# A hybrid decoder layer on one core: the values product of the attention emitted one piece later, and the gate rows' last steps moved behind the attention

## The chip, the cores and the metric

The kernel runs on one core of one Trainium2 chip. The metric is device time in microseconds (us) of one execution, as the median of several. The profile is of one execution; its times count from its first instruction. Engine names: TensorE (PE; its weight loads are listed as PEld), VectorE (DVE), ScalarE (ACT), GpSimd (POOL) and SyncE (SP), which issues all DMAs of this kernel.

## What is computed

One decoder layer over 1024 positions of width 1024, all in 32 bits. Three mixers read the same normalised input: a stick-breaking attention with 8 heads of 64, an mLSTM with 4 heads of 128 in chunks of 128, and a cross-attention into 256 memory tokens. Their outputs are merged by gates and projected, and a gated MLP with a short convolution follows. The change touches the first two:

```python
# stick-breaking attention, one block of 128 queries
z = einsum('bhtd,bhsd->bhts', q[t0:t1], k[:t1]) * scale
log_fail = where(strict, log_sigmoid(-z), 0.0)
log_after = cumsum(log_fail, axis=3, reverse=True) - log_fail
w = where(strict, exp(log_sigmoid(z) + log_after), 0.0)
out = einsum('bhts,bhsd->bhtd', w, v[:t1])
# mLSTM: for each chunk, from the gates i and log f
b = cumsum(lfc);  m_inter = b + m_st
m_t = maximum(m_inter, max(log_d, axis=-1));  w_inter = exp(m_inter - m_t)
m_new = maximum(b_last + m_st, max(b_last - b + ic))
```

## The kernel before

The program is written as Python generators, and a scheduler places the emitted instructions on each engine by the order of emission and by which buffers are free. Every engine then runs its own list strictly in order, so what stands in front of an instruction on its engine holds it. Positions are reversed, so that "later" keys stand at higher block numbers.

**The attention.** Four passes (`for p in range(4)`), each for a pair of heads. A pass has 12 pieces (`PIECES`): a block `rb` of 128 queries against up to four blocks of 128 keys. A piece goes through this chain:

- `sb_weights`: TensorE computes the scores into `z` (L410, L412 adds the mask, L413), two PSUM banks for both heads, one buffer. ScalarE takes two sigmoids of them (L415, L416). VectorE makes the running product by a scan for each head (L422), and multiplies (L424) to the weights `g`.
- `sb_apply`: TensorE transposes `g` block by block into `tr` (L438), ScalarE copies that to `wt` (L440, tile `y`, two buffers), and TensorE multiplies `wt` with the values (L444), accumulating over the pieces of a row of blocks. `store_y` writes four finished blocks out (L395, L396).

Between the pieces stand parts of a dense projection (`chunks`, L149 to L151: three matmuls of 512 columns for each product, since operands are split into a high and a low part): in the first three passes the queries and keys of the next pair of heads, whose evictions are L374 to L377 and L381 to L386. In two pieces of three one such part of 12 matmuls is emitted. The order within a piece is set by the loop: scores, then the part of the projection, then `sb_apply` of the piece before.

**The gate rows.** `gate_rows` computes the mLSTM's decays and maxima, which depend on the input alone, with the 8 chunks x 4 heads on 32 partitions. It is a generator of four steps. The first has the log-sigmoid, the prefix sums and running maxima (`suffix`) and writes their last columns to DRAM (`bl_d`). The second reads them back with heads on partitions (L556) and runs through the chunks, seven dependent instructions on 4 x 1 elements (L561), to `mp_d`. The third reads that back (L567), forms the stabiliser `gm` (L569) and three exponentials (L571, L573, L576), and writes two rows to `me_d` (L577, L578). The fourth transposes three of the tiles (L582) and copies them to `cols` (L583). The mLSTM's chunks (`ml_chunk`) read `me_d` (L843) and `cols` much later.

The steps are called in the attention's first two passes:

```python
            if p < 2 and n in (2, 7):
                next(rows_step)
```

**Behind the attention** come the dense units of `staged` (`seven`: a product of two pairs of weight tiles in seven multiplications). `go(n)` advances them. In them ScalarE and VectorE split each weight tile into a high and a low part (L136, L137) ahead of its 12 matmuls, in two alternating buffers, `whi` and `wlo`.

Of the kernel before, what the change touches and what calls it, by code (L numbers as in the profile page):

```python
# [12 lines left out]
AF = mybir.ActivationFunctionType  # L13
ALU = mybir.AluOpType
# [11 lines left out]
MLH, MLD = 4, 128  # L26
# [3 lines left out]
NCH = S // P  # L30
# [12 lines left out]
def tile_hybrid_layer(ctx: ExitStack, tc: tile.TileContext, xT, memT, vecs, w_t, w_n, w_kv, w_if,  # L43
# [4 lines left out]
    nc = tc.nc  # L48
# [11 lines left out]
    def nm(s):  # L60
        uid[0] += 1
        return f"{s}_{uid[0]}"
# [5 lines left out]
    def T(shape, tag, dt=F32, bufs=None):  # L68
        pool = {"mw": mlp, "mst": mlp, "ga": mlp, "gm": mlp,  "px": late[0]}.get(tag, sb)
        return pool.tile(shape, dt, tag=tag, name=nm(tag), bufs=bufs or BUFS[tag])  # L70
# [7 lines left out]
    def wide():  # L78
        return T([P, S], "U")

    def two(tag):
        return psx[0].tile([P, 2, HALF], F32, tag=tag, name=nm("ps_" + tag), bufs=1)
# [3 lines left out]
    def small(n, p=P):  # L86
        return T([p, n], "sm")

    def bank(tag):
        if tag in ("pj", "pv"):  # L90
            return ps.tile([P, HALF], F32, tag=tag, name=nm("ps_" + tag), bufs=2)
        if px1 is not None:
            if not spare.get(tag):
                t = two(tag)
                spare[tag] = [t[:, 1], t[:, 0]]
            return spare[tag].pop()
        return psx[0].tile([P, HALF], F32, tag=tag, name=nm("ps_" + tag), bufs=2)

    def dtile(shape, name):
        return dr.tile(shape, F32, tag=name, name=name)  # L100
# [4 lines left out]
    def ts(t):  # L105
        return slice(t * P, (t + 1) * P)
# [53 lines left out]
    def rstd(acc, n):  # L160

        nt = n // P
        pc = bank("tr")
        for t in range(nt):
            nc.tensor.matmul(pc[:, t:t + 1], acc[:, ts(t)], ones[:, :1], start=True, stop=True)
        return rstd_cols(pc[:, :nt], nt, D)
# [103 lines left out]
    def x_stats(xp):  # L270
        acc = []
        for i in range(4):
            sq = wide()
            nc.scalar.activation(sq, xp[i], AF.Square)
            acc.append(sq)
            if i:
                nc.vector.tensor_add(acc[0], acc[0], sq)
        a = acc[0][:, hs(0)]
        nc.vector.tensor_add(a, a, acc[0][:, hs(1)])
        return a  # L280
# [10 lines left out]
    pk, pv = [[bank(t) for _ in range(2)] for t in ("z", "pv")]  # L291
# [26 lines left out]
    r = rstd(x_stats(xp[1]), HALF)  # L318
# [74 lines left out]
    def store_y(b, j, h, src_ps):  # L393
        t = T([P, HALF], "me")
        nc.scalar.activation(t, src_ps, AF.Copy)  # L395
        nc.sync.dma_start(y_d[b][j, :, hs(h)], t)  # L396
# [5 lines left out]
    acc_pv = [None]  # L402
# [22 lines left out]
        carry[0] = f[:, :, w:w + 1]  # L425
        return g

    def sb_apply(p, rb, o, g):
        nb = NCH - rb
        m = min(4, nb - o)  # L430
        w = m * P
        if rb % 4 == 3 and o == 0:
            acc_pv[0] = bank("pv")
        pv = acc_pv[0]
        pt = two("tr")
        for a in range(2):
            for j in range(m):
                nc.tensor.transpose(pt[:, a, ts(j)], g[:, a, ts(j)], ident)  # L438
        wt = T([P, 2, HALF], "y")
        nc.scalar.activation(wt[:, :, :w], pt[:, :, :w], AF.Copy)  # L440
        for j in range(m):
            s = rb + o + j
            for a in range(2):
                nc.tensor.matmul(  # L444
                    pv[64 * a:64 * a + 64, ts(rb % 4)],
                    sbv[s // 2][:, s % 2, (2 * p + a) * 64:(2 * p + a + 1) * 64],
                    wt[:, a, ts(j)], start=(o + j == 0), stop=(o + j == nb - 1))
        if rb % 4 == 0 and o + 4 >= nb:
            store_y(0, p, rb // 4, pv)
# [39 lines left out]
    a = x_stats(xp[0])  # L489
    for _ in range(1):  # L490
        next(vals)
    r = rstd(a, HALF)
# [16 lines left out]
    R = NCH * MLH  # L509

    def rows_tile():
        return T([R, P], "mw")
# [12 lines left out]
    cols = const.tile([P, 3, R], F32, tag="cols", name="cols")  # L525

    def gate_rows():
        gi, gf = rows_tile(), rows_tile()
        for g, t in ((0, gi), (1, gf)):
            nc.sync.dma_start(t, if_d[g].rearrange("h (c t) -> c h t", t=P))  # L530

        e = rows_tile()
        nc.scalar.activation(e, gf, AF.Abs)
        nc.scalar.activation(e, e, AF.Exp, scale=-1.0)
        u = rows_tile()
        nc.vector.tensor_scalar(u, e, 1.0, None, op0=ALU.add)
        lu = rows_tile()
        nc.scalar.activation(lu, u, AF.Ln)
        nc.vector.scalar_tensor_tensor(e, u, 1.0, e, op0=ALU.subtract, op1=ALU.subtract)
        nc.vector.reciprocal(u, u)  # L540
        nc.vector.tensor_mul(e, e, u)
        nc.vector.tensor_sub(lu, lu, e)
        bcur = rows_tile()
        nc.vector.scalar_tensor_tensor(bcur, gf, 0.0, lu, op0=ALU.min, op1=ALU.subtract)

        bcum = suffix(bcur, ALU.add)
        ga = T([R, P], "ga", bufs=1)
        nc.vector.tensor_sub(ga, gi, bcum)
        amax = suffix(ga, ALU.max)
        bl_d = dtile([2, R], "bl_d")  # L550
        nc.sync.dma_start(bl_d[0].rearrange("(r o) -> r o", o=1), bcum[:, 0:1])
        nc.sync.dma_start(bl_d[1].rearrange("(r o) -> r o", o=1), amax[:, 0:1])
        yield
        last = small(16, MLH)
        for g in range(2):
            nc.sync.dma_start(last[:, 8 * g:8 * g + 8].rearrange("h (c o) -> h c o", o=1),  # L556
                              bl_d[g].rearrange("(c h o) -> h c o", h=MLH, o=1))
        mp = small(8, MLH)
        nc.vector.memset(mp, 0.0)
        for c in range(NCH - 1, 0, -1):  # L560
            nc.vector.tensor_scalar(mp[:, c - 1:c], mp[:, c:c + 1], last[:, 8 + c:9 + c], last[:, c:c + 1],  # L561
                                    op0=ALU.max, op1=ALU.add)
        mp_d = dtile([NCH, MLH], "mp_d")
        nc.sync.dma_start(mp_d.rearrange("c (h o) -> h c o", o=1), mp.rearrange("h (c o) -> h c o", o=1))
        yield
        mprev = small(1, R)
        nc.sync.dma_start(mprev, mp_d.rearrange("c (h o) -> (c h) o", o=1))  # L567
        gm = T([R, P], "gm", bufs=1)
        nc.vector.tensor_scalar(gm, amax, mprev, -1.0, op0=ALU.max, op1=ALU.mult)  # L569
        ge = rows_tile()  # L570
        nc.scalar.activation(ge, gm, AF.Exp, bias=mprev)  # L571
        gw = rows_tile()
        nc.scalar.activation(gw, ga, AF.Exp, bias=gm[:, 0:1])  # L573
        gfl = rows_tile()
        nc.vector.tensor_sub(gfl, gm, bcum)
        nc.scalar.activation(gfl, gfl, AF.Exp)  # L576
        nc.sync.dma_start(me_d[0], gm)  # L577
        nc.sync.dma_start(me_d[1], ge)  # L578
        yield
        pt = two("tr")[:, 0]  # L580
        for i, t in enumerate((ga, gw, gfl)):
            nc.tensor.transpose(pt[:, i * R:(i + 1) * R], t, ident[:R, :R])  # L582
        nc.vector.tensor_copy(cols.rearrange("p a r -> p (a r)"), pt[:, :3 * R])  # L583
        yield

    rows_step = gate_rows()


# [5 lines left out]
        nc.sync.dma_start(v_d[t], v)  # L594


    ready = []

    def apply_next():
        if ready:  # L600
            sb_apply(*ready.pop(0))

    for p in range(4):
        now = st
        if p < 3:
            st, chunks = sb_qk(p + 1)
            chunks = chunks()
        else:
            chunks = nat_chunks(1, ev_v, [0, 1, 2, 3, 7, 6, 5, 4])
        for n, (rb, o) in enumerate(PIECES):  # L610
            g = sb_weights(p, now, rb, o)
            if n % 3 < 2:
                next(chunks, None)
            if p < 2 and n in (2, 7):
                next(rows_step)
            apply_next()
            ready.append((p, rb, o, g))
        if p < 3:
            for _ in chunks:
                pass  # L620
    apply_next()

    spare.clear()
# [22 lines left out]
    def turn(i, tags):  # L646
        cyc[i] += 1
        return tags[cyc[i] % len(tags)]
# [146 lines left out]
    for g in range(2):  # L795
        for a, b, n in ((0, C_CW, 16), (32, C_CB, 4)):
            nc.vector.tensor_scalar(cw[:, a + g * n:a + (g + 1) * n], col(b + g * n, n), KAP[g], None,
                                    op0=ALU.mult)
# [118 lines left out]
    def go(n):  # L917
        for _ in range(n):
            next(dense, None)
# [4 lines left out]
            next(chunks)  # L924
    go(3)
    LONG[:], SHORT[:] = ["pj"], ["pv"]
    go(24)
    state = [[None], [None]]
    old = []
    for c in range(NCH - 1, -1, -1):  # L930
# [82 lines left out]
    for i in range(3 * KT):  # L1013
        b, n = i // KT, i % KT
# [5 lines left out]
        for h in (1, 0):  # L1020
            p = bank("pj")
            for j in range(4):
                c = slice(((n % 2) * 4 + j) * P, ((n % 2) * 4 + j + 1) * P)
# [104 lines left out]
    for j in range(2):  # L1128
        bl = x1p[2 + j]
        for i in range(2):  # L1130
            nc.vector.scalar_tensor_tensor(bl[:, hs(i)], bl[:, hs(i)], col(C_GFFN + 4 + 2 * j + i), rows,
                                           op0=ALU.mult, op1=ALU.mult)
# [11 lines left out]
    last = first[2]  # L1144
    for u in units[3:]:
# [3 lines left out]
        last = u  # L1149
# [66 lines left out]
    R = [bank(turn(2, LONG)) for _ in range(4)]  # L1216
# [169 lines left out]
```

## Time and profile before

| | |
|---|---|
| median of 3 runs | 1730.78 us (1727.46 to 1735.63) |
| profiled execution | 1730.8 us, span 1728.9 us |
| TensorE busy | 1674.0 us, 97% of the span |
| VectorE busy | 1197.5 us, 69% |
| ScalarE busy | 831.6 us, 48% |
| GpSimd busy | 63.5 us, 4% |

Busy time is the union of an engine's instructions. Matmuls are pipelined, so that two of 0.39 us can start 0.23 us apart, and a TensorE that is shown busy all the time may still lose time between them. The granted clock is the share of TensorE's full clock of 2.4 GHz. The stretch from 114 to 359 us is the attention, and the change concerns it and the 90 us behind it.

### The profile page before, as it was taken

How to read it: one execution, taken by the hardware profiler on the slowest of the kernel's cores; microseconds unless marked ns; L12 is line 12 of the kernel's file. 1: busy time of each engine (PE TensorE's matmuls, PEld its weight loads, DVE VectorE, ACT ScalarE, POOL GpSimd, SP SyncE). 2: the span in 40 equal slices, each digit the busy share in tenths (PEclk: the TensorE clock that was granted, in tenths of full speed). 3: DMA queues.
4: the chain of work that ended last, by engine and by line, in shares of the span. 5: the costliest groups of instructions: out<-in, count | busy, mean ns of one | idle time of the engine just before them, and what ended most of it. 6: DMA issues, size and time to landing. Idle time of an engine off the chain costs nothing.

```text
span 1728.9 us, 21405 instructions
## 1 busy us (share of the span) xinstructions
PE 1674.0 (97%) x7927; PEld 1339.9 (78%) x7927; DVE 1197.5 (69%) x1763; ACT 831.6 (48%) x1298; POOL 63.5 (4%) x139
## 2 busy tenths in 40 slices
PE   8997999999999999999999999999999999999999
PEld 4776777778786777777788888688888888788887
DVE  5555777686973655655546756998788777789874
ACT  4545767554554444555521334465555455544431
POOL 1000000000000121200000000000000000000000
PEclk9998999999999999999999999999999999999999
DMA  8321100162233455532475355143222221496142
GB/s 295 135 63 20 38 19 31 56 195 67 104 143 103 147 174 159 178 116 80 176 256 185 108 176 182 50 135 110 74 74 97 86 73 49 138 355 215 41 140 80
DMA packets 99069, 212.73 MB, mean 123 GB/s; under 512 B 13184, under 2 KB 41088, under 8 KB 98964
## 3 DMA queue, kind: packets, MB, share of 16 engines
q1 hardware_dynamic: 98964, 211.35, 36.6%
q8 instruction: 63, 1.03, 0.3%
q14 instruction: 42, 0.34, 0.1%
HBM read 156.71 MB, written 54.61 MB: 122 GB/s over the span
## 4 chain that ended last, share of the span: by engine, by line
PE 58%; DVE 2%; DMA 1%; ACT 1%; issue 1%; POOL 0%; POOLq 0%; SPq 0%; ACTq 0%; DVEq 0%
PE ps_pj L149 9%; PE ps_pj L151 9%; PE ps_pj L150 9%; PE ps_pv L150 4%; PE ps_pv L151 4%; PE ps_pv L149 4%; PE ps_tr L149 3%; PE ps_tr L151 3%; PE ps_tr L150 3%; PE ps_z L151 2%; PE ps_z L149 2%; PE ps_z L150 2%; PE ps_z L986 1%; PE ps_z L961 1%; DMA raw<-y_d 1%
## 5 line engine op out<-in xcount | busy, mean ns | idle before, releaser
L150 PE MATMUL ps_pj<-h,whi 128*128 128x512 f32 x620 | 244.4, 394 | 0.0
L136 ACT ACTIVATE whi<-raw 128x512 fp32r<-128x512 f32 (+1 forms) x112 | 93.6, 836 | 186.6 <-PE ps_pj L150 80.7
L149 PE MATMUL ps_pj<-h,whi 128*128 128x512 f32 x412 | 163.9, 398 | 0.1
L149 PE MATMUL ps_pj<-pg,whi 128*128 128x512 f32 x396 | 155.6, 393 | 0.0
L151 PE MATMUL ps_pj<-pg,wlo 128*128 128x512 f32 x380 | 148.4, 391 | 0.2 <-DVE wlo L137 0.2
L150 PEld LDWEIGHTS ps_pj<-h,whi 128*128 128x128 f32 x620 | 116.6, 188 | 24.4 <-issue 1.1
L151 PE MATMUL ps_pj<-h,wlo 128*128 128x512 f32 x332 | 131.6, 396 | 0.7 <-DVE wlo L137 0.7
L422 DVE TENSOR_TENSOR_SCAN U<-U 128x512 f32<-128x512 f32 (+3 forms) x96 | 88.6, 965 | 45.6 <-ACT U L415 44.8
L804 DVE SCALAR_TENSOR_TENSOR y<-U,vec,y 128x1023 f32<-128x1023 f32 x88 | 112.6, 1282 | 7.9 <-ACT y L802 7.9
L149 PEld LDWEIGHTS ps_pj<-h,whi 128*128 128x128 f32 x412 | 77.8, 189 | 16.0 <-DVE U L1029 0.8
L137 DVE TENSOR_TENSOR wlo<-raw,whi 128x1024 fp32r<-128x1024 f32 x54 | 66.0, 1222 | 32.6 <-ACT whi L136 32.5
L149 PEld LDWEIGHTS ps_pj<-pg,whi 128*128 128x128 f32 x396 | 74.6, 188 | 17.4 <-issue 1.6
L151 PEld LDWEIGHTS ps_pj<-pg,wlo 128*128 128x128 f32 x380 | 71.3, 188 | 15.7 <-DVE wlo L137 0.6
L136 ACT ACTIVATE whi<-pg 128x512 fp32r<-128x512 f32 (+1 forms) x59 | 43.4, 736 | 73.9 <-PE ps_pv L150 20.0
L150 PE MATMUL ps_pj<-pg,whi 128*128 128x512 f32 x188 | 74.7, 397 | 0.0
L151 PEld LDWEIGHTS ps_pj<-h,wlo 128*128 128x128 f32 x332 | 62.8, 189 | 14.7 <-DVE wlo L137 1.6
L137 DVE TENSOR_TENSOR whi<-raw,whi 128x512 fp32r<-128x512 f32 x58 | 40.1, 691 | 34.9 <-ACT whi L136 34.9
L150 PE MATMUL ps_pv<-h,whi 128*128 128x512 f32 x164 | 63.8, 389 | 0.0
L802 ACT ACTIVATE y<-U,vec 128x1024 f32<-128x1024 f32 x44 | 54.6, 1240 | 14.7 <-DVE U L708 14.7
L151 PE MATMUL ps_pj<-h,whi 128*128 128x512 f32 x156 | 61.4, 394 | 0.0
L415 ACT ACTIVATE U<-ps_z 128x1024 f32<-128x1024 f32 (+3 forms) x48 | 39.0, 813 | 37.1 <-PE ps_z L413 36.9
L137 DVE TENSOR_TENSOR wlo<-raw,wlo 128x512 fp32r<-128x512 f32 x58 | 40.1, 691 | 23.4 <-ACT wlo L136 23.0
(432 smaller groups left out, 4341.9 us busy)
## 6 DMA issues: line engine op xcount, KB each, us to landing
raw<-in_w_t_dram SPq DMA_DIRECT2D x29, 512.0 KB, 3.3
gate_d<-U SPq DMA_DIRECT2D x24, 512.0 KB, 2.6
U<-gate_d SPq DMA_DIRECT2D x24, 512.0 KB, 6.2
pg<-in_w_up_dram SPq DMA_DIRECT2D x22, 512.0 KB, 3.9
act_d<-y SPq DMA_DIRECT2D x22, 512.0 KB, 3.1
pg<-in_w_t_dram SPq DMA_DIRECT2D x21, 512.0 KB, 3.2
raw<-in_w_dn_dram SPq DMA_DIRECT2D x18, 512.0 KB, 4.0
raw<-in_w_o_dram SPq DMA_DIRECT2D x16, 512.0 KB, 4.1
```

The costliest lines, as they stand in the source:

```text
L136: nc.scalar.activation(hi, src, AF.Copy)
L137: (eng or nc.vector).tensor_sub(lo, src, hi.bitcast(F32))
L149: nc.tensor.matmul(out, lh, rh, start=start, stop=False, skip_group_check=more)
L150: nc.tensor.matmul(out, lh, rl, start=False, stop=False, skip_group_check=more)
L151: nc.tensor.matmul(out, ll, rh, start=False, stop=stop, skip_group_check=more)
L415: nc.scalar.activation(f[:, :, 1:w + 1], z[:, :, :w], AF.Sigmoid, scale=-0.125)
L422: nc.vector.tensor_tensor_scan(f[:, a, 1:w + 1], f[:, a, 1:w + 1], f[:, a, 1:w + 1], 1.0 if o == 0 else f[:, a, 0:1], op0=ALU.mult, op1=AL ...
L802: nc.scalar.activation(out, u, AF.Identity, bias=bias, scale=taps[0])
L804: nc.vector.scalar_tensor_tensor(out[:, :S - s], u[:, s:], taps[s], out[:, :S - s], op0=ALU.mult, op1=ALU.add)
L961: nc.tensor.matmul(z[:, i * NMEM:(i + 1) * NMEM], q[:, ts(2 * t2 + i)], kv[:, 0], start=True, stop=True)
L986: nc.tensor.matmul(pv, kv[:, 1, ts(m)], pTs[m], start=(m == 0), stop=(m == 1))
```

## The change

`sb_apply` is cut in two. `sb_turn` does the transposes and the copy, `sb_apply` the product with the values. A piece waits in one list between weights and turn, and in another between turn and product, so that its product is emitted one piece later. Of the gate rows, only step 1 is still called in the attention; steps 2 to 4 are called behind it, among the dense units. The run through the chunks, `gm` and one difference go to GpSimd, the copy to `cols` to ScalarE, and the tile that is read back moves from the small tiles to a part of a wide one.

```diff
-    def sb_apply(p, rb, o, g):
-        nb = NCH - rb
-        m = min(4, nb - o)
+    def sb_turn(rb, o, g):
+        m = min(4, NCH - rb - o)
         w = m * P
-        if rb % 4 == 3 and o == 0:
-            acc_pv[0] = bank("pv")
-        pv = acc_pv[0]
         pt = two("tr")
         for a in range(2):
             for j in range(m):
                 nc.tensor.transpose(pt[:, a, ts(j)], g[:, a, ts(j)], ident)
         wt = T([P, 2, HALF], "y")
         nc.scalar.activation(wt[:, :, :w], pt[:, :, :w], AF.Copy)
+        return wt
+
+    def sb_apply(p, rb, o, wt):
+        nb = NCH - rb
+        m = min(4, nb - o)
+        if rb % 4 == 3 and o == 0:
+            acc_pv[0] = bank("pv")
+        pv = acc_pv[0]
         for j in range(m):
...
-        last = small(16, MLH)
+        last = wide()[:MLH, :16]
...
-        nc.vector.memset(mp, 0.0)
+        nc.gpsimd.memset(mp, 0.0)
         for c in range(NCH - 1, 0, -1):
-            nc.vector.tensor_scalar(mp[:, c - 1:c], mp[:, c:c + 1], last[:, 8 + c:9 + c], last[:, c:c + 1],
+            nc.gpsimd.tensor_scalar(mp[:, c - 1:c], mp[:, c:c + 1], last[:, 8 + c:9 + c], last[:, c:c + 1],
                                     op0=ALU.max, op1=ALU.add)
...
-        nc.vector.tensor_scalar(gm, amax, mprev, -1.0, op0=ALU.max, op1=ALU.mult)
+        nc.gpsimd.tensor_scalar(gm, amax, mprev, -1.0, op0=ALU.max, op1=ALU.mult)
...
-        nc.vector.tensor_sub(gfl, gm, bcum)
+        nc.gpsimd.tensor_sub(gfl, gm, bcum)
...
-        pt = two("tr")[:, 0]
+        pt = bank("tr")
...
-        nc.vector.tensor_copy(cols.rearrange("p a r -> p (a r)"), pt[:, :3 * R])
+        nc.scalar.activation(cols.rearrange("p a r -> p (a r)"), pt[:, :3 * R], AF.Copy)
...
-    ready = []
+    weights, turned = [], []
+
+    def turn_next():
+        if weights:
+            p, rb, o, g = weights.pop(0)
+            turned.append((p, rb, o, sb_turn(rb, o, g)))
 
     def apply_next():
-        if ready:
-            sb_apply(*ready.pop(0))
+        if turned:
+            sb_apply(*turned.pop(0))
...
-            if p < 2 and n in (2, 7):
+            if (p, n) == (0, 2):
                 next(rows_step)
             apply_next()
-            ready.append((p, rb, o, g))
+            turn_next()
+            weights.append((p, rb, o, g))
...
+    apply_next()
+    turn_next()
     apply_next()
...
-    go(24)
+    next(rows_step)
+    go(8)
+    next(rows_step)
+    go(4)
+    next(rows_step)
+    go(12)
```

In the changed file the transposes are L434, the copy L436 and the product L448; the gate rows' read back is L560, the steps through the chunks L565, the second read back L571, the exponentials L575, L577 and L580.

The first place is TensorE's list in the first pass, around the product of its third piece. `ps_tr` holds the transposes, `ps_z` scores, `ps_pj` the projection, `ps_pv` the products with the values from `y`. Before:

```order
L438 MATMUL ps_tr_1032<-ident,U_922 128x128 x6
L410 MATMUL ps_z_1047<-pg_274,pg_272 128x512
L412 MATMUL ps_z_1047<-mask,ident 128x128
L413 MATMUL ps_z_1047<-pg_276,pg_272 128x512
L410 MATMUL ps_z_1047<-pg_275,pg_273 128x512
L444 MATMUL ps_pv_906<-y_1039,pg_548 64x128 x2
L444 MATMUL ps_pv_906<-y_1039,pg_436 64x128 x4
L412 MATMUL ps_z_1047<-mask,ident 128x128
L413 MATMUL ps_z_1047<-pg_277,pg_273 128x512
L149 MATMUL ps_pj_1019<-h_105,whi_858 128x512
```

The product stood four matmuls behind the transposes that it needs, between the scores of a later piece. The same product (`y_1039`) after the change:

```order
L150 MATMUL ps_pj_1015<-h_115,whi_858 128x512
L151 MATMUL ps_pj_1015<-h_107,wlo_859 128x512
L149 MATMUL ps_pj_1015<-h_108,whi_858 128x512
L150 MATMUL ps_pj_1015<-h_116,whi_858 128x512
L151 MATMUL ps_pj_1015<-h_108,wlo_859 128x512
L448 MATMUL ps_pv_990<-y_1039,pg_548 64x128 x2
L448 MATMUL ps_pv_990<-y_1039,pg_436 64x128 x4
L434 MATMUL ps_tr_1078<-ident,U_1008 128x128 x8
L410 MATMUL ps_z_1089<-pg_274,pg_272 128x128
```

It now stands behind all six matmuls of those scores and 12 of the projection, the last five of which are shown, and just ahead of the next piece's transposes.

The second place is SP's list behind the attention, after the change. `w_t` are weights of the dense units, `bl_d`, `mp_d` and `me_d` the gate rows' DRAM tiles:

```order
L691 DMA pg_3163<-in_w_t_dram 128x1024
L560 DMA U_3204<-bl_d 4x8x1 x2
L568 DMA mp_d<-sm_3207 4x8x1
L571 DMA sm_3609<-mp_d 32x1
L581 DMA me_d<-gm_3611 32x128
L582 DMA me_d<-mw_3613 32x128
L855 DMA me_4375<-me_d 128x256
L855 DMA me_4407<-me_d 128x256
L855 DMA me_4375<-me_d 128x256
L855 DMA me_4407<-me_d 128x256
L688 DMA raw_3467<-in_w_t_dram 128x1024
```

Before, the two weight loads at its ends followed each other here; the gate rows' DMAs stood in the first pass of the attention, and the four reads of `me_d` just behind the attention.

The third place is ScalarE's list, a little later, after the change:

```order
L707 ACTIVATE U_3233<-ps_tr_3079 128x512
L136 ACTIVATE wlo_3287<-pg_3120 128x512
L575 ACT_TABLE_LOAD
L575 ACTIVATE mw_3613<-gm_3611,sm_3609 32x128
L136 ACTIVATE whi_3302<-hf_3157 128x512
L577 ACTIVATE mw_3615<-ga_964,gm_3611 32x128
L580 ACTIVATE mw_3617<-mw_3617 32x128
L712 ACTIVATE U_3233<-ps_tr_3079 128x512
```

Before, the two splits (L136) followed each other here. The table load waits for the second read back (`sm_3609`), its exponential for `gm`, and a split for the dense units stands behind both.

## Rows read from the trace of the kernel before

**Rows 1.** Third pass, window: length, PE, PEld, DVE, ACT, POOL busy, clock, DMA

```profile
241.00:298.00 57.00, 53.66 (x378) 42.04 (x377) 41.75 (x51) 37.36 (x53) 0.82 (x8) 1.00 0.08 29
```

**Rows 2.** TensorE's timeline (start, length; [idle before]): four passes' starts, two waits

```profile
114.43 0.22 PE L410 MATMUL ps_z<-pg,pg 128*128 128x128 f32 x1
...
143.39 1.94 PE L438 MATMUL ps_tr<-ident,U 128*128 128x128 f32 x8 [3.04 <-DVE U L420]
...
158.75 0.58 PE L410 MATMUL ps_z<-pg,pg 128*128 128x256 f32 x1 [4.80 <-ACT U L416]
...
184.98 0.22 PE L410 MATMUL ps_z<-pg,pg 128*128 128x128 f32 x1
...
241.38 0.22 PE L410 MATMUL ps_z<-pg,pg 128*128 128x128 f32 x1
...
298.39 0.22 PE L410 MATMUL ps_z<-pg,pg 128*128 128x128 f32 x1
```

**Rows 3.** Timeline of SP, VectorE and ScalarE at the gate rows' steps

```profile
133.75 0.25 SPq L556 DMA_DIRECT2D sm<-bl_d  x1
...
138.19 1.45 DVE L561 TENSOR_SCALAR sm<-sm,sm 4x1 f32<-4x1 f32 x5 [4.05 <-DMA sm<-bl_d]
...
143.51 0.25 SPq L564 DMA_DIRECT2D mp_d<-sm  x1
...
148.62 0.32 SPq L567 DMA_DIRECT2D sm<-mp_d  x1
...
153.75 1.28 ACT L571 ACT_TABLE_LOAD   x1 [7.30 <-DMA sm<-mp_d]
155.04 0.40 ACT L571 ACTIVATE mw<-gm,sm 32x128 f32<-32x128 f32 x1
```

**Rows 4.** Windows around the two waits of rows 2

```profile
143.00:150.00 7.00, 6.61 (x33) 5.60 (x34) 4.28 (x9) 1.02 (x1) 0.00 (x0) 0.54 0.62 28
158.00:164.00 6.00, 5.25 (x22) 4.11 (x23) 4.69 (x7) 5.66 (x9) 0.00 (x0) 0.57 0.00 0
```

**Rows 5.** Waits in 112 to 360 us: total us, times, longest

```profile
PE ps_pv L444 <- ACT y L440: 8.5, 24, 0.6
PEld ps_pv L444 <- ACT y L440: 22.8, 42, 1.0
```

**Rows 6.** Timeline of two pieces in the third pass

```profile
265.40 0.39 PE L150 MATMUL ps_pj<-h,whi 128*128 128x512 f32 x1
...
266.35 0.85 PEld L444 LDWEIGHTS ps_pv<-y,pg 128*64 128x64 f32 x16 [0.99 <-ACT y L440]
266.36 1.09 PE L444 MATMUL ps_pv<-y,pg 128*64 128x128 f32 x16 [0.56 <-ACT y L440]
...
267.38 1.09 PE L438 MATMUL ps_tr<-ident,U 128*128 128x128 f32 x8
...
268.57 1.02 ACT L440 ACTIVATE y<-ps_tr 128x1024 f32<-128x1024 f32 x1 [0.48 <-PE ps_tr L438]
```

**Rows 7.** Timeline of the dense units behind the attention

```profile
382.31 0.38 SPq L679 DMA_DIRECT2D pg<-in_w_t_dram  x1
...
401.62 0.63 ACT L136 ACTIVATE whi<-hf 128x512 fp32r<-128x512 f32 x1 [1.60 <-PE ps_pv L151]
...
402.29 0.69 DVE L137 TENSOR_TENSOR whi<-hf,whi 128x512 fp32r<-128x512 f32 x1 [1.54 <-ACT whi L136]
...
403.92 0.19 PEld L149 LDWEIGHTS ps_pj<-pg,whi 128*128 128x128 f32 x1
...
414.45 0.33 SPq L676 DMA_DIRECT2D raw<-in_w_t_dram  x1
```

**Rows 8.** Window behind three weight loads

```profile
386.00:388.00 2.00, 2.00 (x10) 1.68 (x9) 1.97 (x4) 1.15 (x2) 0.00 (x0) 1.00 0.43 174
```

**Rows 9.** GpSimd's groups by line: count | busy us, mean ns | idle before

```profile
L157 POOL TENSOR_TENSOR sm<-sm,nhalf 128x2 f32<-128x2 f32 x17 | 12.9, 758 | 48.7 <-DVE sm L155 34.3 <-DVE sm L891 14.4
L418 POOL MEMSET U<- 128x2 f32 x32 | 3.2, 102 | 213.1 <-PE ps_tr L438 149.6 <-DVE U L420 37.6 <-DVE U L424 15.4
```

## The prediction

> **What bounds the kernel now.** I read first the granted clock and the busy times of one undisturbed pass of the attention (a pass is one of its four pairs of heads, cut into 12 pieces), then TensorE's waits in order of time, then what ended them, and last the place behind the attention to which steps are moved.
>
> In the third pass TensorE is busy 53.66 of 57 us at full clock, VectorE 41.75, ScalarE 37.36 [rows 1]: TensorE sets the pace, and the other two have a quarter and more of their time free. Passes begin where the scores of their first piece begin: 114.43, 184.98, 241.38 and 298.39 [rows 2]. So the first pass takes 70.55 us, the second 56.40, the third 57.01. The first pass is 13.5 us longer than the third, and in it lie two holes, 3.04 us at 143.39 and 4.80 us at 158.75 [rows 2].
>
> Rows 3 say what stands behind the holes. The gate rows read back a small DRAM tile: issued at 133.75, used by VectorE at 138.19, which had idled 4.05 us with the piece's scans queued behind the waiting instruction. Those scans feed the transposes of 143.39. Then the chunk maxima go out at 143.51, the read back can be issued only at 148.62, and its data let ScalarE go on at 153.75, after 7.30 us of idling. ScalarE's sigmoid of the next scores stands behind, and TensorE waits for it until 158.75.
>
> The clock makes each hole dearer. It is 0.54 on average in 143 to 150 and 0.57 in 158 to 164 [rows 4]. With levels of 1.0 and 0.5 (2.4 and 1.2 GHz) that is 1.2 GHz for 7 x 0.46 x 2 = 6.44 us and 6 x 0.43 x 2 = 5.16 us, so until 149.44 and 163.16, each time after TensorE had idled.
>
> The second loss is spread over all passes. The first product with the values waits for ScalarE's copy of the transposed weights: 8.5 us over 24 waits by the matmuls, 22.8 us over 42 by the weight loads [rows 5].
>
> **The gate rows' steps, gain.** Their waits go from VectorE's and ScalarE's queues in the attention. The holes are 3.04 + 4.80 = 7.84 us. TensorE worked at 1.2 GHz from 143.39 to 149.44 and from 158.75 to 163.16, 6.05 + 4.41 us, and half of that comes back: 5.2. Sum 13.0 us, which agrees with the 13.5 us between the passes. I take 13.0, with bounds 11 (only the 7.84 and a part of the clock) and 14. Step 1, with its prefix sums, stays where it was.
>
> **The values product, gain.** What does one wait cost? The matmul of 265.40 takes the next one 0.23 us later in a full stream (0.39 us long, overlapped), but the values product begins at 266.36: 0.73 us lost, where the matmul's column says 0.56 and the loader's 0.99 [rows 6]. The loss is half way between the columns, so for all waits (8.5 + 22.8) / 2 = 15.7 us.
>
> The order before puts the product four matmuls behind its transposes, within the next piece's scores. The new order puts it behind those scores and, in two pieces of three, behind 3 to 12 matmuls of the projection, at 0.23 us each. The copy takes 1.02 us and starts 0.1 us behind the transposes (268.47 to 268.57) when ScalarE is free, so some 1.3 us of other work hide it. By the built order nine of a pass's twelve pieces have 1.9 us or more (in the last pass its last three have less). The first (0.8 us of work), the fourth (0.5) and the seventh (1.7, but the copy stands behind four key evictions on ScalarE) still wait. I let these 12 of 48 keep 0.73 us each, 8.8 us. Gain 15.7 - 8.8 = 6.9, taken as 7. Bounds: 1 (what is freed turns into waits of the transposes for VectorE) and 15.7 (all of it). I stay in the middle because the scores, no longer cut in two by the waiting product, finish earlier, so that VectorE's chain starts earlier too.
>
> **The gate rows' steps, cost at the new place.** No row shows this chain there, so I build it. SP is free at 382.69 and its next issue is at 414.45 [rows 7], so 31.8 us of SP's queue are empty. The read back goes out at 382.7. DMA is still 43% busy in 386 to 388 [rows 8], until about 386.9. From issue to first use took 4.4 us in rows 3 (133.75 to 138.19): the data are there between 387.1 (nothing queued ahead) and 391.3 (all of it ahead). I take 388.5.
>
> Seven dependent steps on GpSimd follow, an operation of which no row shows a single one there. Bounds: 102 ns (its small memset) and 758 ns (its power on 2 columns) [rows 9], so 0.7 to 5.3 us for seven. I take 0.3 us each, near VectorE's five in 1.45 us, since one column of work is nearer to the memset: 2.1. The write and the read back took 143.51 to 148.62 and 148.62 to 153.75 [rows 3], 10.2 us. So the data reach ScalarE's new exponential at 400.8, between 398.0 and 406.8.
>
> On ScalarE that exponential stands ahead of the split of 401.62, and behind it wait VectorE's difference and TensorE's weight load of 403.92. The difference ends at 402.98 [rows 7], so there are 0.94 us to spare: the split may start at 402.56. The exponential takes a table load of 1.28 us and 0.40 us more [rows 3], so the data must be there by 400.8 or 400.9. My estimate lies on the edge. I charge 1 us; the bounds are 0 and 406.8 - 400.8 = 6.0, with 2.2 us for a half clock as after the second hole, 8.2 together.
>
> Rows 3 show the exponential starting at 155.04, with the end of its table load (153.75 + 1.28). The Trainium skill (ScalarE: Activation LUTs, What ACT_TABLE_LOAD costs) counts about 2.66 us for a switch, a drain of 1.38 us included; the trace does not agree, since nothing lies between the two. By that rule the sum would be about 1.4 us higher, 1713.
>
> Behind the exponential SP sends both gate rows and reads them for the chunks: with 5.1 us from a write to the read of it, as in rows 3, it is done near 409.5, 5 us before the weight load of 414.45. The transposes and the copy to the columns (ScalarE's now) come later still, and I charge nothing: both stood among the attention's work before, and nothing but ScalarE's next split waits there. Without that cover it is the copy, some 0.4 us by the exponential of rows 3. The other table loads leave ScalarE in the attention, and are in the 13.0.
>
> **Sum.** 13.0 + 7 - 1 = 19 us from the profiled execution of 1730.8 us (span 1728.9, 1.9 around it), which is also the median shown (1730.78): 1711.8, so 1712.
>
> **Rivals.** (1) The values waits only change their name: TensorE comes earlier to the transposes and waits there for VectorE's multiplication. For it: a pass that shortens raises VectorE's load. Against it: VectorE is idle 15 of 57 us [rows 1]. Gain 13 + 1 - 1, so 1718.
>
> (2) The data for the exponential come at the late bound, 406.8: the read back queues behind all the weight loads, and a GpSimd step costs as much as its power, 0.758 us [rows 9]. TensorE then stops for 6.0 us at the weight load of 403.92, and the half clock takes 2.2: without the charge of 1 the sum is 1710.8, and with 8.2 in its place 1719. For it: two of my three terms of that chain are from far rows. The Trainium skill (GPSIMD Engine Reference, Instruction dispatch) states an approximately 6 us load of code at the first call of a freshly loaded GpSimd kernel, with no instruction in the profile; by it alone the data would come at 406.8 too. Rows 9 show nothing of that size, but hold no first call of this operation.
>
> (3) All waits of the values product go: 13.0 + 15.7 - 1, so 1703.
>
> (4) Slower: the seven dependent GpSimd steps hold ScalarE. Each microsecond by which their data pass 400.8 stops TensorE for one. At 0.3 us a step they take 2.1; the gain of 20 is used up once the stop is 17.8 us (with 2.2 for the clock), so 19.9 us for seven, 2.85 us a step. Beyond 4.1 us a step the kernel is over 0.5% slower; at 4.5 it takes 1742. The longest small step of rows 9 is 0.758 us.
>
> **How the numbers follow.** Forecast (1706 to 1716) 0.54; rival 1 0.18; rival 2 0.10; rival 3 0.12; rival 4 0.03; little change from causes not listed 0.03. The likeliest is 1712. 1702 to 1722 takes in rivals 1 to 3 and both bounds of the values product, and leaves out about 0.1. About 0.5%, 8.7 us, can be told from no change, so faster means under 1722.1: the forecast, rivals 1 and 3 and a part of rival 2 where the data come a little earlier, 0.87. Within 0.5%: 0.10. Slower: 0.03.
>
> **What would show it.** Right: the clock stays at 1.0 from 114 to the attention's end; no hole of TensorE over 2 us in the first pass, which falls under 59 us; the waits of the values product for the copy fall to about 12 to 16, most in first, fourth and seventh pieces; waits of the transposes for VectorE grow by less than 3 us. At the new place: the data before the exponential arrive about 18 us after the first read back is issued, and a wait of TensorE there of 0 to 2 us. Wrong: GpSimd steps near 1 us, a hole behind the exponential with the clock at 0.5, or transposes that take over the waits of the values product.

## The result and the profile after

The changed kernel takes 1708.4 us in the median (1704.7 to 1713.2) against 1730.5: a ratio of 0.9871 (95% interval 0.9836 to 0.9906), so 22 us less, where 19 were forecast. Its profiled execution has a span of 1705.4 us, against 1728.9.

The timeline of TensorE answers to [rows 2]: where the passes start, the attention's last product, and the longest idle time that is left.

```profile
114.38 0.22 PE L410 MATMUL ps_z<-pg,pg 128*128 128x128 f32 x1
119.87 0.39 PE L410 MATMUL ps_z<-pg,pg 128*128 128x256 f32 x1 [1.02 <-ACT U L416]
...
168.01 0.33 PE L410 MATMUL ps_z<-pg,pg 128*128 128x128 f32 x1
...
221.56 0.33 PE L410 MATMUL ps_z<-pg,pg 128*128 128x128 f32 x1
...
276.09 0.33 PE L410 MATMUL ps_z<-pg,pg 128*128 128x128 f32 x1
...
333.09 1.09 PE L448 MATMUL ps_pv<-y,pg 128*64 128x128 f32 x16
```

The first pass takes 53.63 us (70.55 before), the second 53.55 (56.40), the third 54.53 (57.01). The two holes are gone. The windows, with the columns of [rows 1], have the clock at 1.00 in every pass:

```profile
114.00:168.00 54.00, 51.22 (x344) 40.37 (x342) 47.24 (x84) 39.64 (x55) 2.44 (x8) 1.00 0.11 34
168.00:221.50 53.50, 52.50 (x377) 41.68 (x376) 41.61 (x51) 37.34 (x52) 2.65 (x10) 1.00 0.09 31
221.50:276.00 54.50, 53.50 (x382) 42.32 (x380) 42.54 (x52) 38.26 (x55) 0.92 (x9) 1.00 0.09 31
```

The waits in 112 to 336 us answer to [rows 5]. The product waits for its copy for 4.0 and 10.6 us, where it was 8.5 and 22.8; the transposes wait for VectorE's multiplication for 1.0.

```profile
PEld ps_pv L448 <- ACT y L436: 10.6, 18, 0.9
PE ps_pv L448 <- ACT y L436: 4.0, 12, 0.5
PE ps_tr L434 <- DVE U L424: 1.0, 2, 0.7
```

The gate rows' chain at its new place, in the timelines of SP, GpSimd, ScalarE and TensorE (with one of its weight loads, PEld); it answers to [rows 3] and [rows 7]:

```profile
356.20 0.64 SPq L560 DMA_DIRECT2D U<-bl_d  x2
...
361.03 7.41 POOL L565 TENSOR_SCALAR sm<-sm,U 4x1 f32<-4x1 f32 x7 [46.87 <-DMA U<-bl_d]
...
368.46 0.24 SPq L568 DMA_DIRECT2D mp_d<-sm  x1
371.54 0.32 SPq L571 DMA_DIRECT2D sm<-mp_d  x1
...
375.59 1.28 ACT L575 ACT_TABLE_LOAD   x1 [1.71 <-DMA sm<-mp_d]
376.88 0.40 ACT L575 ACTIVATE mw<-gm,sm 32x128 f32<-32x128 f32 x1
377.19 0.62 ACT L136 ACTIVATE whi<-hf 128x512 fp32r<-128x512 f32 x1
...
377.77 0.19 PEld L149 LDWEIGHTS ps_pj<-pg,whi 128*128 128x128 f32 x1
...
383.44 0.39 PE L149 MATMUL ps_pj<-pg,whi 128*128 128x512 f32 x1
```

From the first read back to its data 4.8 us, seven steps 7.4 us (1.06 us each), write and read back 7.1, so 19.4 us in all. TensorE does not wait between 360 and 395 us. The split behind the exponential ends at 377.81, and the matmul that takes its result starts at 383.44, 5.6 us later. It cannot be the matmul of 378.00, which also reads a `whi`: the load of its weights starts at 377.77, before that split ends.

Where did the 23.5 us of span come from? This is the attention's last product in the kernel before:

```profile
357.98 1.09 PE L444 MATMUL ps_pv<-y,pg 128*64 128x128 f32 x16
```

In the changed kernel it starts at 333.09, 24.9 us earlier. Counted by the same ScalarE instructions behind it, the lead is 26.1 us at 356.5, 26.8 at 433, 25.7 at 587 and 23.9 at 624.5. The last of these losses falls together with the clock. These are windows around a wait for GpSimd (L865, before L853) in the mLSTM, first of the changed kernel, then of the kernel before.

```profile
618.00:622.00 4.00, 2.09 (x11) 1.69 (x10) 2.74 (x6) 1.70 (x4) 1.48 (x4) 0.83 0.60 221
622.00:626.00 4.00, 4.00 (x15) 3.19 (x15) 0.35 (x1) 1.12 (x2) 0.00 (x0) 0.75 0.47 168
```

```profile
642.00:646.00 4.00, 2.08 (x13) 1.49 (x11) 1.77 (x7) 1.70 (x4) 1.28 (x3) 1.00 0.75 247
646.00:650.00 4.00, 4.00 (x22) 3.46 (x23) 1.65 (x4) 1.12 (x2) 0.72 (x1) 1.00 0.51 173
```

TensorE waits there for 1.91 us after and 1.92 before. Only after did the clock fall behind it, to 0.83 and 0.75: 4 x 0.17 x 2 + 4 x 0.25 x 2 = 3.4 us at half clock, 1.7 us lost.

This fall is not what tells the two spans apart, though. Behind the attention the clock falls twice in each of the two traces, and each fall costs 1.7 us: in the kernel before between 444 and 452 us (the first two windows) and between 1104 and 1112 (0.65 and 0.92), in the changed kernel at 621 us and between 1080 and 1088 (the last two).

```profile
444.00:448.00 4.00, 3.27 (x10) 2.17 (x11) 4.00 (x6) 3.90 (x6) 0.00 (x0) 0.80 0.01 5
448.00:452.00 4.00, 4.00 (x15) 3.23 (x14) 4.00 (x5) 0.04 (x1) 0.00 (x0) 0.77 0.32 128
```

```profile
1080.00:1084.00 4.00, 3.47 (x8) 2.25 (x9) 4.00 (x5) 2.00 (x3) 0.00 (x0) 0.68 0.01 4
1084.00:1088.00 4.00, 4.00 (x17) 3.25 (x16) 4.00 (x5) 1.03 (x1) 0.00 (x0) 0.90 0.00 0
```

### The profile page after: what moved, and what is told of

It is laid out like the page before. It is cut to its first block, busy times and chain, and to the rows that moved or that the text cites. A ratio compares the mean times of both kernels' runs of the same rounds, so it can differ in the third digit from the quotient of the medians.

```text
span 1705.4 us, 21424 instructions
## 1 busy us (share of the span) xinstructions
PE 1666.4 (98%) x7927; PEld 1334.5 (78%) x7927; DVE 1195.2 (70%) x1752; ACT 824.4 (48%) x1293; POOL 72.0 (4%) x149
## 4 chain that ended last, share of the span: by engine, by line
PE 58%; DMA 2%; DVE 2%; ACT 2%; issue 1%; POOL 0%; POOLq 0%; SPq 0%; ACTq 0%; DVEq 0%
PE ps_pj L149 8%; PE ps_pj L151 8%; PE ps_pj L150 8%; PE ps_pv L150 4%; PE ps_pv L149 4%; PE ps_pv L151 4%; PE ps_tr L149 3%; PE ps_tr L150 3%; PE ps_tr L151 3%; PE ps_z L150 2%; PE ps_z L149 2%; PE ps_z L151 2%; DMA raw<-y_d 1%; PE ps_z L1003 1%; PE ps_z L978 1%
## 5 line engine op out<-in xcount | busy, mean ns | idle before, releaser
L136 ACT ACTIVATE whi<-raw 128x512 fp32r<-128x512 f32 (+1 forms) x112 | 93.6, 836 | 189.2 <-PE ps_pj L150 86.2
L422 DVE TENSOR_TENSOR_SCAN U<-U 128x512 f32<-128x512 f32 (+3 forms) x96 | 88.6, 964 | 31.3 <-ACT U L415 30.4
L149 PEld LDWEIGHTS ps_pj<-pg,whi 128*128 128x128 f32 x396 | 74.3, 188 | 17.3 <-issue 1.6
L136 ACT ACTIVATE whi<-pg 128x512 fp32r<-128x512 f32 (+1 forms) x59 | 43.4, 737 | 75.1 <-PE ps_pv L150 20.1
L436 ACT ACTIVATE y<-ps_tr 128x1024 f32<-128x1024 f32 (+3 forms) x48 | 39.0, 813 | 39.0 <-PE ps_tr L434 38.7
L137 DVE TENSOR_TENSOR wlo<-raw,wlo 128x512 fp32r<-128x512 f32 x58 | 40.0, 690 | 24.1 <-ACT wlo L136 23.9
```

The lines of the kernel that those rows point to most:

```text
L136: nc.scalar.activation(hi, src, AF.Copy)
L137: (eng or nc.vector).tensor_sub(lo, src, hi.bitcast(F32))
L149: nc.tensor.matmul(out, lh, rh, start=start, stop=False, skip_group_check=more)
L422: nc.vector.tensor_tensor_scan(f[:, a, 1:w + 1], f[:, a, 1:w + 1], f[:, a, 1:w + 1], 1.0 if o == 0 else f[:, a, 0:1], op0=ALU.mult, op1=AL ...
```

## Experiments

All times are medians, and the ratios are to the kernel before, measured on the same chip (1731 to 1732 us). Gains over the kernel before are worked out from the ratios. The diffs are cut to the lines that matter.

**The later product alone.** The two calls of the steps, and the steps, as before (against the changed kernel):

```diff
-            if (p, n) == (0, 2):
+            if p < 2 and n in (2, 7):
                 next(rows_step)
```

> The values product is emitted one piece later, as in the changed kernel; the gate rows' steps stay in the attention as before. By the prediction's sum the later product is worth 7 us (bounds 1 to 15.7): 1724 us. The profiles read by pass say more: passes two to four each became 2.5 to 2.9 us shorter, which over four passes is about 10 us: 1720. Rival: the attention's holes grow, because the first pass's spare time is used by the gate rows' round trips, and little of it is seen: 1727 or more. The two holes of the first pass, 3.0 and 4.8 us, should both still be there, with the half clock behind them.

1718.7 us, ratio 0.9922 (0.9906 to 0.9937): 13.5 us less, more than any of the figures expected. The last three passes run 51.80, 54.56 and 58.06 us where they had 56.40, 57.01 and 60.69, and the first 66.58 where it had 70.55. TensorE's timeline, with the attention's first scores, the two holes and the last product:

```profile
115.95 0.22 PE L410 MATMUL ps_z<-pg,pg 128*128 128x128 f32 x1
...
143.80 1.08 PE L434 MATMUL ps_tr<-ident,U 128*128 128x128 f32 x8 [3.11 <-DVE U L420]
...
159.50 0.80 PE L410 MATMUL ps_z<-pg,pg 128*128 128x512 f32 x1 [3.12 <-ACT U L416]
...
345.85 1.09 PE L448 MATMUL ps_pv<-y,pg 128*64 128x128 f32 x16
```

The second hole is 3.12 us where it was 4.80: the later product gives TensorE something to do while ScalarE waits. So the later product also shortens what the gate rows cost.

**The gate rows alone.** The product behind its transposes as before, the steps behind the attention (the call of the steps, against the kernel before):

```diff
-            if p < 2 and n in (2, 7):
+            if (p, n) == (0, 2):
                 next(rows_step)
```

> Only the gate rows' steps 2 to 4 are moved behind the attention, partly to GpSimd; the values product stands as before. By the prediction 13.0 us of gain and 1 of cost: 1718 to 1719. The first pass became 16.95 us shorter in the changed kernel; without the 2.6 us by which the others shrank that is 14.3, and so about 1716. Rival: the two edits need each other, and the holes are only filled where the later product gives the transposes room: then 1722 or more. The waits of the values product for the copy should stay at 30 us (loads and matmuls together).

1717.7 us, ratio 0.9924 (0.9909 to 0.9939): 13.2 us less. TensorE's timeline and its waits:

```profile
114.82 0.22 PE L410 MATMUL ps_z<-pg,pg 128*128 128x128 f32 x1
...
171.59 0.22 PE L410 MATMUL ps_z<-pg,pg 128*128 128x128 f32 x1
...
228.38 0.22 PE L410 MATMUL ps_z<-pg,pg 128*128 128x128 f32 x1
...
344.66 1.09 PE L444 MATMUL ps_pv<-y,pg 128*64 128x128 f32 x16
```

```profile
PEld ps_pv L444 <- ACT y L440: 26.1, 44, 1.0
PE ps_pv L444 <- ACT y L440: 11.4, 30, 0.6
```

The first pass takes 56.77 us, as long as the second (56.79): all of the 13.8 us are in the first. The waits of the product did not stay at 31.3 us but rose to 37.5: by passes, from 4.6 to 8.4 in the first and from 8.3 to 10.5 in the second, the two passes in which the steps had stood; the other two kept theirs.

**The steps on VectorE again**, behind the attention:

```diff
-            nc.gpsimd.tensor_scalar(mp[:, c - 1:c], mp[:, c:c + 1], last[:, 8 + c:9 + c], last[:, c:c + 1],
+            nc.vector.tensor_scalar(mp[:, c - 1:c], mp[:, c:c + 1], last[:, 8 + c:9 + c], last[:, c:c + 1],
...
-        nc.gpsimd.tensor_scalar(gm, amax, mprev, -1.0, op0=ALU.max, op1=ALU.mult)
+        nc.vector.tensor_scalar(gm, amax, mprev, -1.0, op0=ALU.max, op1=ALU.mult)
...
-        nc.gpsimd.tensor_sub(gfl, gm, bcum)
+        nc.vector.tensor_sub(gfl, gm, bcum)
```

> The changed kernel with the run through the chunks, the stabiliser and the difference on VectorE again, at the same place behind the attention. If GpSimd's 1.06 us per step are wholly hidden and VectorE's 0.29 too, nothing moves: 1708, within 2 us. Rival: on VectorE they stand among the splits of the dense units, the stabiliser waits there for its read back, and a split behind it is late: 1710 to 1714, with a new wait of TensorE of 2 us or more between 375 and 395 us.

1709.3 us, ratio 0.9871 (0.9856 to 0.9885), the same as the changed kernel's. That the steps run on GpSimd is worth nothing here. The timelines of ScalarE and of the weight loads:

```profile
380.83 1.28 ACT L575 ACT_TABLE_LOAD   x1 [4.04 <-DMA sm<-mp_d]
...
384.35 0.19 PEld L149 LDWEIGHTS ps_pj<-pg,whi 128*128 128x128 f32 x1 [0.49 <-ACT U L707]
```

The data come 5.24 us later than in the changed kernel, 4.56 of them against TensorE's work, which runs 0.68 us later in this trace (the matmul of 378.00 starts at 378.68). TensorE is then 0.23 us late: the matmul of 383.44 starts at 384.35, where its distance from the matmul of 378.00 gives 384.12. So 4.3 us were to spare.

**The steps in the attention, on GpSimd**, with the later product; the tile read back and the copy to `cols` are those of the kernel before:

```diff
-            if (p, n) == (0, 2):
+            if p < 2 and n in (2, 7):
                 next(rows_step)
...
-    next(rows_step)
-    go(8)
-    next(rows_step)
-    go(4)
-    next(rows_step)
-    go(12)
+    go(24)
```

> The later product, the gate rows' steps in the attention as before, but with the run through the chunks, the stabiliser and the difference on GpSimd in place of VectorE. If the first hole (3.1 us at 143.80 in the run of the later product alone) comes from VectorE's queue standing behind the read back, it goes; the second (3.1 us at 159.50), which comes from ScalarE's exponential behind the second read back, stays. That is 3.1 us and some 3 of half clock less than 1718: 1712 to 1714. Rival: GpSimd sets the first element of the running products (its memsets stand behind its steps), so the hole only moves to that engine: 1718.

1720.9 us, ratio 0.9937 (0.9912 to 0.9961), not faster than with VectorE (0.9922). The timelines of ScalarE and TensorE show why:

```profile
150.22 1.28 ACT L575 ACT_TABLE_LOAD   x1 [10.85 <-DMA sm<-mp_d]
...
153.35 1.98 PE L448 MATMUL ps_pv<-y,pg 128*64 128x128 f32 x16 [8.66 <-ACT y L436]
```

The first hole is gone, as expected, but in the built order the exponential now stands ahead of a piece's copy. ScalarE waits 10.85 us for the second read back, and TensorE 8.66 in one piece. The rival that I had named (GpSimd's memsets behind its steps) is not what happened. A wait taken from one in-order queue came back, longer, in another; of the two places tried, the one behind the attention takes both away.

**The run through the chunks twice**, and then **eight times**, so that the data come later:

```diff
-        for c in range(NCH - 1, 0, -1):
+        for c in 2 * list(range(NCH - 1, 0, -1)):
```

> The changed kernel with GpSimd's run through the chunks done twice over (14 dependent steps in place of 7; the result is the same), so that the data of the second read back reach ScalarE 7.4 us later, near 383 us. By the prediction each microsecond past the edge stops TensorE for one, and the changed kernel's split ended 0.2 us before the matmul that takes it: a stop of some 7 us, and 2 for the half clock behind it, so 1717. Rival: the edge is not there, other work fills the time, and the time stays at 1708 to 1710.

1709.7 us, ratio 0.9867 (0.9851 to 0.9884): no loss. The second seven steps add only 3.7 us (14 take 11.13), the data come at 379.91, 4.3 us later (3.6 against TensorE's work), and the scheduler put the exponential one split further back. The edge was not where the prediction saw it.

> The changed kernel with GpSimd's run through the chunks done eight times over (56 dependent steps; the result is the same). The run with 14 steps brought the data of the second read back to ScalarE 4.3 us later and cost nothing. Read again, the split behind the exponential (377.19 in the changed kernel) is not taken by TensorE at 378.00 but one pair of units later, at 383.44: 5 us to spare. With steps of 0.35 to 0.53 us the 56 end between 386 and 392 us and the data come at 393 to 399; behind them stand an eviction and a split that TensorE takes near 387. So a stop of 9 to 15 us and 2 for the half clock: 1720 to 1725. Rival: the scheduler puts the exponential behind the splits that would be late, and nothing is lost: 1708 to 1710.

1726.5 us, ratio 0.9969 (0.9951 to 0.9988): 18 us over the changed kernel. The timelines of GpSimd, ScalarE and TensorE, and the windows behind the stop:

```profile
362.64 26.03 POOL L565 TENSOR_SCALAR sm<-sm,U 4x1 f32<-4x1 f32 x56 [47.54 <-DMA U<-bl_d]
...
395.98 1.28 ACT L575 ACT_TABLE_LOAD   x1 [18.95 <-DMA sm<-mp_d]
397.27 0.40 ACT L575 ACTIVATE mw<-gm,sm 32x128 f32<-32x128 f32 x1
...
399.69 0.80 PE L149 MATMUL ps_pj<-pg,whi 128*128 128x512 f32 x1 [15.17 <-ACT U L707]
```

```profile
398.00:402.00 4.00, 2.31 (x6) 1.83 (x7) 2.58 (x4) 2.68 (x7) 0.41 (x1) 0.50 0.57 93
402.00:406.00 4.00, 4.00 (x15) 3.23 (x14) 0.64 (x2) 1.12 (x2) 0.41 (x1) 0.77 0.17 42
```

The data are 20.4 us later than in the changed kernel, 19.5 of them against TensorE's work (the matmul of 378.00 starts at 378.92), and TensorE stops for 15.2. So 4.3 us were to spare, as with the steps on VectorE, and past them a microsecond costs a microsecond. The clock is 0.50 from the stop to about 403.8 (4 x 0.23 x 2 = 1.84 us at half into the second window), which takes another 2.1 us: 17.3 of the 18. What is late first is not the split, which now stands ahead of the exponential, but an eviction (L707) behind it: it reads out the PSUM bank to which TensorE's next product adds.

**Even parts of the projection.** Parts of 6 matmuls (of 12 before), two behind the first piece of three and one behind each of the others:

```diff
-                if k == 3:
+                if k in (1, 3, 5):
                     yield
...
-            if n % 3 < 2:
+            for _ in range((2, 1, 1)[n % 3]):
                 next(chunks, None)
```

> The changed kernel with the projection cut into parts of 6 matmuls in place of 12, emitted 2, 1, 1 over three pieces in place of 2, 2, 0 of such parts, so that every product with the values has at least 6 matmuls (1.36 us) of the projection behind the scores and ahead of it. The waits that are left in the changed kernel (4.0 us of matmuls and 10.6 us of weight loads, 7.3 us by half) are mostly those of the first, fourth, seventh and tenth pieces, whose product has no part ahead of it. If that is why, they fall to 4 us or less in sum, and the time by 4 to 6 us, to 1703. Rival: TensorE then waits for VectorE's multiplication at the transposes instead, whose spare time was 0.15 to 0.6 us in the ninth and twelfth pieces: 1708.

1699.3 us, ratio 0.9813 (0.9791 to 0.9835): 9 us below the changed kernel, and the fastest here. The waits:

```profile
PEld ps_pv L448 <- ACT y L436: 0.9, 2, 0.5
PE ps_tr L434 <- DVE U L424: 0.6, 3, 0.2
```

So what was left of the product's waits was the missing part ahead of every third product. In the trace 5.2 us of the gain lie in the attention, as expected: from its first scores to the end of its last product it takes 214.7 us (115.12 to 329.77), in the changed kernel 219.8 (114.38 to 334.18). Behind the attention the clock stays at 1.00 to the end of the work, where it fell twice in the changed kernel, 1.7 us each time. Whether the even parts are why it did not fall was not shown.

**The transposes ahead of the product**, in the changed kernel, and then with even parts:

```diff
-            apply_next()
             turn_next()
+            if len(turned) > 1:
+                apply_next()
             weights.append((p, rb, o, g))
```

> The changed kernel with the next piece's transposes ahead of the product in place of behind it, so that 1.1 us of transposes cover the copy where no projection part does. The waits of the product should vanish as in the run with even parts (up to 7 us less). Against it: the transposes come up to 1.1 us earlier, and TensorE waits for VectorE where the multiplication had ended only 0.15 to 0.6 us ahead, in three pieces of a pass: 12 x 0.6 = 7 us. I expect 1705 to 1710, and the waits to move from the product to the transposes.

1712.9 us, ratio 0.9891 (0.9872 to 0.9910), some 4 us over the changed kernel by the medians, though the two intervals overlap. In the traces its attention takes 226.7 us against 219.8. The waits:

```profile
PEld ps_tr L434 <- ACT y L436: 7.2, 10, 1.1
PE ps_tr L434 <- DVE U L424: 4.0, 5, 1.6
PE ps_tr L434 <- ACT y L436: 2.2, 6, 0.5
```

Besides the wait for VectorE, which was expected, there is one that was not: the transposes have one PSUM buffer (`two` gives one for each name), so they wait for the copy of the piece before to have read it.

> Even parts and the transposes ahead of the product together. If the product's waits are gone with even parts alone, nothing more is to be had here, and the earlier transposes cost: 1703 to 1708, not below the run with even parts alone. Rival: the two together give the copy the longest cover, and the last weight loads' waits go too: 1701.

1706.1 us, ratio 0.9852 (0.9830 to 0.9873): 7 us above even parts alone, so the order of the changed kernel, product first, is the better one.

## Why the prediction was right, point by point

**Gate rows, 13.0.** Right, and for the reason given. Alone, with the cost at the new place in it, the move gives 13.2 us; the trace has 13.8 in the first pass and less than half a microsecond in the others. Both holes came from engines that stood in order behind a round trip to DRAM; the run with the steps on GpSimd in the attention shows that another engine for the steps does not help there.

**Values product, 7 with bounds 1 to 15.7.** The mechanism was right, the term too small. Alone it is worth 13.5 us, and on top of the moved gate rows 1717.7 - 1708.4 = 9.3. The prediction halved the waits of the kernel before, 15.7, and let 8.8 stay. Two things were off. The waits to be removed were (26.1 + 11.4) / 2 = 18.8, since the gate rows' steps in the first two passes had covered some, as the run with the gate rows alone shows; and (10.6 + 4.0) / 2 = 7.3 stayed. That makes 11.5, and the pass lengths of the two traces differ by 3.1, 3.2, 2.3 and 2.5, 11.1 in sum. So half of the two columns was a good price for these waits. They stayed where they were looked for, and in the tenth pieces: in the first pass TensorE idles for 0.31, 0.55, 0.30 and 0.15 us ahead of the products of the first, fourth, seventh and tenth pieces, which have only 1, 1, 3 and 5 matmuls of the projection between the scores and the product. Even parts took them away.

**The sum.** The two edits do not quite add up. From its first scores to the end of its last product the attention takes 244.6 us before, 231.0 with the later product alone, 230.9 with the gate rows alone and 219.8 with both: 13.7, 13.7 and 24.8 us less. So 2.5 us are in both of the single gains. Of these, 1.6 are the holes, which the later product alone had shortened from 7.84 to 6.23 us; the rest was not traced. The times give 13.5 + 13.2 = 26.7 against 22.3. What is left of that difference is not in the attention. In the traces each of the two single runs has one fall of the clock behind it, at 1.7 us, where the kernel before and the changed kernel have two, so a part of the single gains is the clock's. That the edits caused it was not shown, and with intervals of 3 to 6 us to either side, how much of it is chance stays open.

**New place, 1.** The step that failed here is the reading of the spare time. The split of 401.62 was paired with the weight load of 403.92 [rows 7]; its matmuls stand one pair of units later, which is the 5.6 us seen above between split and matmul. In the kernel before they start with this weight load, 6.4 us behind the end of VectorE's difference (402.98), not 0.94:

```profile
409.36 0.19 PEld L149 LDWEIGHTS ps_pj<-pg,whi 128*128 128x128 f32 x1
```

So the cost was 0, and by two runs the data could have come another 4.3 us later: 23.7 us behind the read back, where 18.1 was taken for the edge. The chain's own terms were off in both directions: 1.06 us a step where 0.3 was taken and 0.758 was the upper bound, 4.8 instead of 5.8 for the first read, and 7.1 instead of 10.2 for write and read back. 19.4 us against 18.1 came of it by cancellation. I had listed GpSimd steps near 1 us as a sign of a wrong prediction; the sign came, and cost nothing.

**The rivals.** The waits did not turn into waits of the transposes (1.0 us, rival 1). The data were not late (rival 2), and waits of 7.3 us stayed (rival 3). The slower case (rival 4) has the right mechanism: with 56 steps its stop appears, one for one. With the spare time as measured it would need 5.6 us more of delay than was worked out.

**The two rules.** The table load lasts 1.28 us and the exponential starts at its end, at 376.88 after, and at 397.27 with 56 steps, as in [rows 3]. The Trainium skill (ScalarE: Activation LUTs, What ACT_TABLE_LOAD costs) counts a drain besides; no run here shows one between the two. GpSimd's seven steps add up to 7.41 us in the first run through, and 49 more took 26.03 - 7.41 = 18.6, 0.38 each, so the first seven are dearer by some 4.7 us. With the steps in the attention the first seven took only 4.46, so the excess is no fixed amount. The Trainium skill (GPSIMD Engine Reference, Instruction dispatch) speaks of about 6 us, with no instruction in the profile; here the extra time stands inside the instructions' own records. That it is the same thing was not shown.

## What to carry to other kernels

When an in-order engine waits for a round trip to DRAM, move the whole chain to where every engine that touches it has time; another engine for its steps only moved the wait here. What a move behind other work costs is decided by the spare time of what stands next in the queue, so follow each such tile to the very matmul that reads it. A product that needs a copy of what was just transposed wants the same amount of other matmuls ahead of it in every piece: two even parts did more than one large part in two pieces of three.

## What was not expected of the hardware

GpSimd's small step took 1.5, 1.2, 1.2, 0.35, 1.3, 0.7 and 0.7 us in its first seven calls, and 0.38 us in the mean of 49 behind the first seven in the run with 56; with the steps in the attention four of the first seven took 0.35. And the same wait of 1.9 us in the mLSTM left the clock at 1.00 in one trace and took it to 0.83 and 0.75 in another, with TensorE busy for 2.08 and 2.09 us of the 4 around it; what decides it was not found.
